# Products on parts of TensorE's array in blocks and groups, with no whole-array product inside a block

## The chip, the cores and the metric

The kernel runs on one core of a Trainium2 chip. The metric is the time of one execution in microseconds (us); lower is better. A core has five engines that each work through their own list of instructions in order: TensorE (PE) multiplies matrices, VectorE (DVE) and ScalarE (ACT) do elementwise work, GpSimd (POOL) does elementwise work and issues the gathers, SyncE (SP) issues the plain transfers. They wait for each other by semaphores only. The array of PE has 128 rows and 128 columns; a product can use all of it, or a part of 32 or 64 rows or columns (its tile size), and products on different parts can run side by side.

## The reference

One step of a hybrid decoder with DEPTH = 2 layers, for 512 prompt tokens and 8 sequences of 8 sample tokens with 2048 cached tokens each, D_MODEL = 1024. A layer is

```python
h = rms_norm(x, p["norms"][0]) * (1.0 + sc1) + sh1          # sc1, sh1, ...: silu(c) @ w_ada
nq, nkv, ngt, ucv, ret, gdn, mg = split_cols(h @ p["w_in"], IN_SPLITS)
o_nsa, new_win = nsa_attention(...)      # compressed, selected and window attention, 4 heads of 64
o_conv, new_conv = conformer_conv(...)   # depthwise convolution, 31 taps
o_ret, new_ret = retention(...)          # chunkwise, 4 heads of 64
o_gdn, ... = gated_deltanet(...)         # chunkwise delta rule, 4 heads of 64
merged = jnp.einsum('btnw,nwd->btnd', branches, p["w_branch"])
gates = jax.nn.sigmoid(mg.reshape(B, T, N_BRANCH, D_MODEL))
mixed = jnp.einsum('btnd,btnd->btd', gates, merged) @ p["w_out"]
x = x + gt1 * rms_norm(mixed, p["norms"][1])
h2 = rms_norm(x, p["norms"][2]) * (1.0 + sc2) + sh2
f, new_ffn = conv_ffn(h2, ...)           # d_ff 2816
x = x + gt2 * rms_norm(f, p["norms"][3])
```

The large products (w_in, w_branch, w_out, the ffn) are whole-array work; heads of 64, blocks of 32 and sums over rows are work on parts of the array.

## The kernel before

**Large products.** Tokens stand in two halves of 288 (512 prompt and 64 sample). Each large product is three products of split numbers, high by high, low by high and high by low (lines 346 to 348 of `mm`), with the weights as 128x128 tiles. `split_w` loads a weight tile `raw`, copies its high part `whi` on ACT (line 298) and subtracts the low part `wlo` on DVE (line 299). Such a product is called an `mm` here.

**Products on part of the array.** 4384 of the program's 18616 matmuls have a tile size smaller than 128x128: sums over rows for the norms (line 415), the pieces of the adaLN product `adaps` in four strips of 32 columns (line 383), retention (lines 833 to 855), the delta rule (1055 to 1223), and most of the attention.

**Order.** The program is written stage by stage with generators that yield between steps; at each yield some products of another stage (the gates and merges of the layer, whose operands are early) can be put between. A scheduler then fixes one static order for each engine from the dependencies, its own durations and priorities. Some helpers add dependencies that set the order only and wait for nothing at run time: `in_one_go` ties the matmuls of one `with` to the first, `after_pe` ties them behind the matmul before, `order_allocs` keeps the buffers of a tag in program order.

**The attention stage (nsa).** It comes last among the four mixers and lies between two stretches of large products; 912 `mm` of gates and merges are at hand there per layer as filling. The prompt part runs 16 steps: scores (line 1617), bias, maximum, exp and scale on DVE and ACT (1621 to 1628) for two heads in turn, transposes of `E` (1634), a copy to `ET` (621), products with the values (1641). The sample part multiplies queries with gathered pages (1662), then with window pages `kwin` (1711), runs a softmax chain `chain(G)` for each of two groups G, and `values(G)` transposes the probabilities (1792) and multiplies them with gathered pages `pg<-cv` (1802). All pages share one tag of 8 buffers; POOL issues one gather per page, 32 of them for `cv` in a layer. The stage ends with line 1813; the last merge, whose first product reads `bh`, needs its result.

Of the kernel before, what the change touches and what calls it, by code (L numbers as in the profile page):

```python
# [46 lines left out]
FCH = [(0, 7), (7, 14), (14, 22)]  # L47

# [125 lines left out]
class Kern:  # L174
    def __init__(self, ctx, tc, ap, depth=DEPTH, dbg=None, mixers=True):
# [14 lines left out]
        self.first = None  # L190

# [44 lines left out]

    def order_after(self):
# [37 lines left out]
    def turn(self, out, src, ident, p=0):  # L275

        if p:
            self.nc.tensor.matmul(out, src, ident, start=True, stop=True)
        else:
            self.nc.tensor.transpose(out, src, ident)  # L280
# [87 lines left out]
    def ada_piece(self, l, q, k, box, mod, par):  # L368
# [9 lines left out]
        def end():  # L378
            if k == 0:
                box.append(self.ax("adaps"))  # L380
            ps = box[0]
            for b in range(4):
                nc.tensor.matmul(ps[32 * b:32 * b + 32, :], self.csil[:, k, :], t[:, 512 * b:512 * b + 512],  # L383
                                 start=k == 0, stop=k == KT - 1, tile_position=(0, 32 * b))
# [5 lines left out]
            for j in range(4):  # L390
                nc.tensor.transpose(po[:, j * P:(j + 1) * P], y[:, j * P:(j + 1) * P], self.ident)
# [12 lines left out]
    def inv_rms(self, srcs, nh, scale, sel, get):  # L404
# [8 lines left out]
        for j, t in enumerate(srcs):  # L413
            for g in range(n):
                nc.tensor.matmul(th[32 * g:32 * g + 32], mat, t[:, g * w:(g + 1) * w], start=j == 0, stop=j == len(srcs) - 1,
# [10 lines left out]
        if n * w == HALF:  # L426
# [4 lines left out]
            nc.tensor.matmul(out[0][:, :HALF], self.ones, own, start=True, stop=True)  # L431
            return [out[0][:, :HALF]]
        for g in range(n):
            c = g * w
            nc.tensor.matmul(out[c // HALF][:, c % HALF:c % HALF + w], sel[:, g * P:(g + 1) * P], r, start=True, stop=True)
# [197 lines left out]
    def proj_tm(self, l, c0, n, h, dst, extra=None):  # L633
# [5 lines left out]
        for tt in range(5):  # L639
# [4 lines left out]
            for k in range(KT):  # L644
                hi, lo = ws[k // 4]
                ah, al = h[k]
                nc.tensor.matmul(o, ah[:, s], hi[:, k % 4], start=k == 0, stop=False)  # L647
                nc.tensor.matmul(o, al[:, s], hi[:, k % 4], start=False, stop=False)  # L648
                nc.tensor.matmul(o, ah[:, s], lo[:, k % 4], start=False, stop=k == KT - 1)  # L649
# [13 lines left out]
    def colsum(self, mat, srcs, hf):  # L663

        ps = self.ps("a", 4)
        for i, t in enumerate(srcs):
            self.nc.tensor.matmul(ps[:, :HALF], mat, t[:, HS[hf]], start=i == 0, stop=i == len(srcs) - 1)
# [114 lines left out]
    def retention(self, l, par, h, rv, qraw, kraw, tick):  # L782
# [4 lines left out]
        with self.phase("rrot", True):  # L787
            perm, cos, sin = self.ctile("perm"), self.ctile("cos"), self.ctile("sin")
            for raw, dst in ((qraw, q), (kraw, k)):
                for p in range(2):  # L790
# [3 lines left out]
                    for hf in range(2):  # L794
                        s = HS[hf]
                        ps = self.ps("a", 2)
                        nc.tensor.matmul(ps[:, :HALF], perm, src[:, s], start=True, stop=True)
# [6 lines left out]
        with self.phase("rchunk", True):  # L804
# [4 lines left out]
            for tt in range(5):  # L809
# [6 lines left out]
                if tt < 4:  # L816
                    for p in range(2):
                        nc.tensor.transpose(ps[:, p * P:(p + 1) * P], k[p][:, s], self.ident)
# [9 lines left out]
                with self.in_one_go():  # L828
                    for p in range(2):
                        for e in range(2):  # L830
                            b = 64 * e
                            oo = pe[e][:, p] if tt < 4 else pe[e][64 * p:64 * p + 64, 0, :SMP]
                            nc.tensor.matmul(oo, k[p][b:b + 64, s], q[p][b:b + 64, s], start=True, stop=True)
# [6 lines left out]
                if tt < 4:  # L840
                    po = self.ps("o", 1)
                    oo = lambda hd: po[64 * (hd % 2):64 * (hd % 2) + 64, hd // 2 * P:(hd // 2 + 1) * P]
                    with self.in_one_go():
                        for hd in (1, 0, 3, 2):
                            nc.tensor.matmul(oo(hd), v[:n, hd * 64:hd * 64 + 64], att[:n, self.hx(hd), :n], start=hd < 2 or tt == 0, stop=tt == 0)
                        if tt:
                            for hd in (1, 0, 3, 2):
                                p, b = hd // 2, 64 * (hd % 2)
                                nc.tensor.matmul(oo(hd), S[p][b:b + 64, :], qx[p][b:b + 64, s], start=False, stop=p == 1)
# [3 lines left out]
                    for hd in range(4):  # L853
                        p, b = hd // 2, 64 * (hd % 2)
                        nc.tensor.matmul(pS[b:b + 64, p * 64:p * 64 + 64], t[:, hd * 64:hd * 64 + 64], v[:, hd * 64:hd * 64 + 64],
# [31 lines left out]
    def on_state(self, out, x, S0, s):  # L887

        for e, p in ((0, 0), (1, 1), (0, 1), (1, 0)):
            b, c = 64 * e, 64 * p  # L890
            self.nc.tensor.matmul(out[e][c:c + 64, :], x[p][b:b + 64, s], S0[p][b:b + 64].rearrange("p b e -> p (b e)"),
# [12 lines left out]
    def sample_state(self, l, S0, dst, o, att, v, kz, q, mask, update, ps, tags=("vx0", "vx1", "oT")):  # L904
# [6 lines left out]
        for p in range(2):  # L911
            b = 64 * p
            for e in range(2):
                nc.tensor.matmul(pa[b:b + 64, e * HD:(e + 1) * HD], att[b:b + 64, e, :SMP], v[b:b + 64, e * HD:(e + 1) * HD],
# [4 lines left out]
        nc.tensor.transpose(pt[:, :P], oT, self.ident)  # L919
# [9 lines left out]
        for e, p in ((0, 0), (1, 1), (0, 1), (1, 0)):  # L929
            b, c = 64 * p, 64 * e  # L930
            nc.tensor.matmul(pS[p][c:c + 64, :], kz[b:b + 64, e * HD:(e + 1) * HD], vx[e][b:b + 64], start=True, stop=True)
# [4 lines left out]
    def gdn(self, l, par, h, tok, feed):  # L936
# [34 lines left out]
        nc.tensor.matmul(ps[:, 0:16], triu, g[:, 0:16], start=True, stop=True)  # L971
        nc.tensor.matmul(ps[:, 32:48], self.ones, g[:, 0:16], start=True, stop=True)
        for b in (0, 64):
            nc.tensor.matmul(ps[b:b + 64, 16:18], triu8[b:b + 64], g[b:b + 64, 16:18], start=True, stop=True)
            nc.tensor.matmul(ps[b:b + 64, 48:50], on8[b:b + 64], g[b:b + 64, 16:18], start=True, stop=True)
# [55 lines left out]
        with self.phase("gchunk", True):  # L1031
# [7 lines left out]
            def inverse(tt, lane):  # L1039
# [13 lines left out]
                for j, hd in enumerate(HDJ):  # L1053
                    gcol = col(g, hd) if pr else g[rows(j), 16 + j // 2:17 + j // 2]
                    nc.tensor.matmul(un(GB, j), gcol.to_broadcast([n, n]), tu[rows(j)], start=True, stop=True)
# [12 lines left out]
                for e in range(2):  # L1068
# [3 lines left out]
                    for p in range(2):  # L1072
                        r, c = rows(p), p if pr else 0
                        nc.tensor.matmul(ps[r, c, :n], k[p][b:b + 64, s], k[p][b:b + 64, s], start=True, stop=True)
                        nc.tensor.matmul(ps[r, w + c, :n], k[p][b:b + 64, s], q[p][b:b + 64, s], start=True, stop=True)
# [18 lines left out]
                def mm32(out, lhsT, rhs, r, c):  # L1094
                    nc.tensor.matmul(out, lhsT, rhs, start=True, stop=True, tile_position=(32 * r, 32 * c))  # L1095
# [40 lines left out]
                if pr:  # L1136
# [26 lines left out]
                    for j in range(4):  # L1163
                        nc.tensor.matmul(ps[h1, j], U[h0, j, h1], X64[h0, j], start=True, stop=True)
# [3 lines left out]
                    for j in range(4):  # L1168
                        nc.tensor.matmul(ps[h0, j], R[h1, j], WT[h1, j, h1], start=True, stop=True)
# [4 lines left out]
            def scan(tt):  # L1174
# [5 lines left out]
                for p in range(2):  # L1180
                    nc.tensor.transpose(ps[:, p * P:(p + 1) * P], k[p][:, s], self.ident)
                    nc.tensor.transpose(ps[:, 256 + p * P:256 + (p + 1) * P], v[p][:, s], self.ident)
# [1066 lines left out]
```

## Time and profile before

| | |
|---|---|
| median of 3 runs | 2560.45 us (2560.42 to 2568.15) |
| the profiled execution | 2563.72 us, span of its instructions 2561.9 us |
| mean granted TensorE clock | 0.988 of full speed |
| PE busy | 2446.2 us, 95% of the span, 22850 matmul records |
| DVE, ACT, POOL busy | 55%, 37%, 24% |

A share of busy time is a mean over many stages. A matmul is shown with a modelled end: an `mm` of 288 columns is shown as about 0.30 us long, though the next one starts 0.13 us after it. So for PE the distance from start to start says more than the length. A matmul in f32 is two passes and leaves two records.

### The profile page before, as it was taken

To read this page: it belongs to the slowest core of one execution; us is meant where nothing else is said; L and a number is where in the kernel's file an instruction comes from. 1 tells how busy PE (TensorE), PEld (TensorE's weight loads), DVE (VectorE), ACT (ScalarE), POOL (GpSimd) and SP (SyncE) were. 2 spreads that over 40 slices of the span, in tenths; PEclk is the share of its full clock that TensorE was granted. 3 is DMA by queue.
4 is the path that set the end of the run, shared out by engine and by line. 5 is a ranking of instruction groups with operands and counts; after the bars stand their busy time and mean duration, and the time that the engine had idled before them with its cause. 6 is when DMAs were issued, how large, how long until landed. Compare 5 with 4: busy or idle time off the path is not lost.

```text
span 2561.9 us, 54461 instructions
## 1 busy us (share of the span) xinstructions
PE 2446.2 (95%) x22850; PEld 2178.6 (85%) x22850; DVE 1411.1 (55%) x2918; ACT 938.0 (37%) x1815; POOL 613.5 (24%) x801
## 2 busy tenths in 40 slices
PE   6999999999999999999989999999999999999997
PEld 3769787976789899999977687889677999999997
DVE  5789644445524662534579884443553357444446
ACT  4316222434324543323452342233442355333233
POOL 2102322235522210101122032322635222000012
PEclk8999999999999999999999999999999999999999
DMA  8753355423634132422467433524345233233234
GB/s 313 228 195 120 111 173 196 141 89 113 198 98 156 54 120 87 144 86 83 129 216 243 139 102 128 172 80 130 108 138 172 93 117 123 84 121 109 88 89 128
DMA packets 125637, 346.78 MB, mean 135 GB/s; under 512 B 28652, under 2 KB 48112, under 8 KB 119184
## 3 DMA queue, kind: packets, MB, share of 16 engines
q1 hardware_dynamic: 104592, 275.05, 33.0%
q0 software_dynamic: 20800, 68.25, 8.3%
q8 instruction: 180, 2.95, 0.5%
q14 instruction: 65, 0.53, 0.1%
HBM read 330.77 MB, written 20.73 MB: 137 GB/s over the span
## 4 chain that ended last, share of the span: by engine, by line
PE 78%; DVE 9%; DMA 5%; ACT 3%; issue 3%; POOL 2%; SPq 0%; ACTq 0%; DVEq 0%; POOLq 0%
PE mm L346 20%; PE mm L347 20%; PE mm L348 19%; DMA pg<-cv,ix 2%; PE x L1095 2%; DVE wlo L299 2%; PE adaps L383 1%; PE cmps L1514 1%; DVE cvy L715 1%; DMA raw<-wout 1%; PE mmt L649 1%; PE mmt L647 1%; PE mmt L648 1%; PE t L1634 1%; DMA raw<-wtr 1%
## 5 line engine op out<-in xcount | busy, mean ns | idle before, releaser
L346 PE MATMUL mm<-hh,whi 128*128 128x288 f32 x3136 | 946.1, 302 | 7.3 <-ACT whi L298 4.5
L347 PE MATMUL mm<-hl,whi 128*128 128x288 f32 x3136 | 938.5, 299 | 1.2 <-DVE hl L483 1.1
L348 PE MATMUL mm<-hh,wlo 128*128 128x288 f32 x3136 | 937.5, 299 | 2.1 <-DVE wlo L299 2.1
L299 DVE TENSOR_TENSOR wlo<-raw,whi 128x1024 fp32r<-128x1024 f32 (+1 forms) x320 | 390.5, 1223 | 534.1 <-ACT whi L298 528.9
L346 PEld LDWEIGHTS mm<-hh,whi 128*128 128x128 f32 x3136 | 591.6, 189 | 36.1 <-issue 14.9
L347 PEld LDWEIGHTS mm<-hl,whi 128*128 128x128 f32 x3136 | 595.2, 190 | 15.0 <-issue 9.3
L348 PEld LDWEIGHTS mm<-hh,wlo 128*128 128x128 f32 x3136 | 592.3, 189 | 17.2 <-issue 11.6
L298 ACT ACTIVATE whi<-raw 128x1024 fp32r<-128x1024 f32 (+1 forms) x320 | 334.9, 1048 | 544.3 <-PE mm L347 354.5
L348 PE MATMUL mm<-acth,wlo 128*128 128x288 f32 x704 | 206.5, 295 | 2.1 <-DVE wlo L299 2.1
L347 PE MATMUL mm<-actl,whi 128*128 128x288 f32 x704 | 208.1, 296 | 0.0
L346 PE MATMUL mm<-acth,whi 128*128 128x288 f32 x704 | 208.0, 296 | 0.1
L576 POOL COPY nfp<-gb 128x2 f32<-128x2 f32 x44 | 42.3, 960 | 610.6 <-ACT gb L550 610.6
L1473 POOL DMA_INDIRECT pg<-ck,ix x128 | 131.1, 1024 | 102.9 <-issue 49.4
L1857 POOL TENSOR_TENSOR f<-f,gate 128x288 f32<-128x288 f32 x80 | 72.4, 919 | 291.3 <-DVE gate L1856 290.7
L348 PEld LDWEIGHTS mm<-acth,wlo 128*128 128x128 f32 x704 | 131.9, 188 | 2.9 <-DVE wlo L299 2.6
L347 PEld LDWEIGHTS mm<-actl,whi 128*128 128x128 f32 x704 | 132.9, 189 | 0.9 <-DVE actl L355 0.5
L346 PEld LDWEIGHTS mm<-acth,whi 128*128 128x128 f32 x704 | 132.2, 188 | 1.3 <-ACT acth L354 1.0
L1473 POOL DMA_INDIRECT fil<-cc,ix x64 | 69.2, 1082 | 143.9 <-PE cmps L1514 125.8
L715 DVE SCALAR_TENSOR_TENSOR cvy<-cgb,par,cvy 128x512 f32<-128x512 f32 x120 | 93.4, 791 | 0.0
L1835 ACT ACTIVATE gate<-mm 128x288 f32<-128x288 f32 x112 | 45.3, 404 | 126.0 <-PE mm L348 105.2
L346 PE MATMUL mm<-bh,whi 128*128 128x288 f32 x256 | 80.1, 315 | 1.9 <-ACT ga L1835 1.4
L347 PE MATMUL mm<-bl,whi 128*128 128x288 f32 x256 | 78.5, 307 | 2.3 <-DVE bl L355 2.3
(600 smaller groups left out, 3965.6 us busy)
## 6 DMA issues: line engine op xcount, KB each, us to landing
raw<-wtr SPq DMA_DIRECT2D x124, 512.0 KB
raw<-wup SPq DMA_DIRECT2D x104, 512.0 KB
f<-wada SPq DMA_DIRECT2D x32, 1024.0 KB
fil<-wada SPq DMA_DIRECT2D x16, 1024.0 KB
raw<-wdn SPq DMA_DIRECT2D x32, 512.0 KB
raw<-wdn SPq DMA_DIRECT2D x32, 448.0 KB
raw<-wbr SPq DMA_DIRECT2D x16, 512.0 KB
raw<-wout SPq DMA_DIRECT2D x16, 512.0 KB
```

What stands on the lines that cost most here:

```text
L298: nc.scalar.activation(hi, raw, AF.Copy)
L299: nc.vector.tensor_sub(lo, raw, hi.bitcast(F32))
L346: nc.tensor.matmul(ps, hi[:, k0 + k], ah[:, s], start=first, stop=False)
L347: nc.tensor.matmul(ps, hi[:, k0 + k], al[:, s], start=False, stop=False)
L348: nc.tensor.matmul(ps, lo[:, k0 + k], ah[:, s], start=False, stop=last)
L383: nc.tensor.matmul(ps[32 * b:32 * b + 32, :], self.csil[:, k, :], t[:, 512 * b:512 * b + 512], start=k == 0, stop=k == KT - 1, tile_positi ...
L576: nc.gpsimd.tensor_copy(newp[:, ft], g[:, SEQ:SEQ + 2])
L715: nc.vector.scalar_tensor_tensor(y[:, :SEQ], gb[:, j:j + SEQ], wj(j), y[:, :SEQ], op0=OP.mult, op1=OP.add)
L1095: nc.tensor.matmul(out, lhsT, rhs, start=True, stop=True, tile_position=(32 * r, 32 * c))
L1473: self.nc.gpsimd.indirect_dma_start(out=dst, out_offset=None, in_=self.ap[src], in_offset=bass.IndirectOffsetOnAxis(ap=ix[:, l, b, j:j + 1 ...
L1835: self.nc.scalar.activation(gts[hf], ps, AF.Tanh, scale=0.5)
L1857: nc.gpsimd.tensor_add(fm, fm, gm)
```

## The change

All matmuls and transposes outside `mm` go through two helpers, which number blocks: a block is a run of products on part of the array that stand together in the program. `issue_together` then adds dependencies that set the order only. The first product of a block stands behind every instruction of another engine that makes an operand of the block or frees its output; the rest of the block stands behind the first. The string GROUPS names 27 groups of neighbouring blocks. In a group each block's first product stands behind the operands of all blocks of the group, and the later blocks get a priority that puts them next. No work is added or taken away; both programs have 18616 matmuls.

```diff
+GROUPS = "3+7+8+9+10+11 12+13 24+26+27 50+52 56+57 68+69+74 70+71 85+86 87+88+89+90 91+92 103+105 112+113 155+157 167+168 212+228 213+214 ..."
+    def mmul(self, out, lhsT, rhs, **k):
+        with self.place(lhsT):
+            self.nc.tensor.matmul(out, lhsT, rhs, **k)
+    def place(self, held):
+        part = held.shape[0] <= 64 or math.prod(held.shape[1:]) <= 64
+        ins = self.nc.cur_bb.bb.instructions
+        if part and (len(ins) in self.cuts or not self.part(ins[-1])):
+            self.block += 1
+            part = self.block in self.later
+        return self.tc.high_priority(10 ** 6) if part else nullcontext()
+    def issue_together(self):
...
+        for group in (*self.groups, *([b] for b in sorted(alone))):
+            need = {u: None for b in group for u in needs[b]}
+            for b in group:
+                for u in need:
+                    self.tc.add_manual_dep(blocks[b][0], u, info, reason="operands of the group")
+        for first, *rest in blocks:
+            for i in rest:
+                self.tc.add_manual_dep(i, first.name, info, reason="in one go")
...
-                                self.nc.tensor.matmul(S[kv], w[rows[kv]], x[rows[kv], :nk], start=j == 0, stop=j == 2)
+                                self.mmul(S[kv], w[rows[kv]], x[rows[kv], :nk], start=j == 0, stop=j == 2)
...
+        self.issue_together()
         self.order_allocs()
```

In the changed program the helpers' lines 246 and 250 stand for all these products, and lines 346 to 348 have become 412 to 414, so rows are told apart by the names of their tiles.

PE, attention over the prompt, second block of queries, before: `s` are scores, `t<-cst,E` the transposes of the probabilities, `o<-ET` the products with the values, `mm` the filling.

```order
L1617 MATMUL s_6571<-nkh,nqh_5699 128x256 x2
L1634 MATMUL t<-cst,E 128x128 x2
L1617 MATMUL s_6571<-nkl,nqh_5699 128x256 x2
L1617 MATMUL s_6571<-nkh,nql 128x256 x2
L1634 MATMUL t<-cst,E 128x128 x2
L348 MATMUL mm<-hh,wlo 128x288
L346 MATMUL mm<-hh,whi 128x288
L347 MATMUL mm<-hl,whi 128x288
L348 MATMUL mm<-hh,wlo 128x288
L1641 MATMUL o<-ET,kvb_6106 64x128 x2
L1641 MATMUL o<-ET,kvb_6134 64x128 x2
```

The same step now:

```order
L250 MATMUL t<-cst,E 128x128 x2
L414 MATMUL mm<-hh,wlo 128x288
L412 MATMUL mm<-hh,whi 128x288
L413 MATMUL mm<-hl,whi 128x288
L414 MATMUL mm<-hh,wlo 128x288
L246 MATMUL o<-ET,kvb_6106 64x128 x2
L246 MATMUL s_6571<-nkh,nqh_5699 128x256
L246 MATMUL o<-ET,kvb_6134 64x128
L246 MATMUL s_6571<-nkh,nqh_5699 128x256
L246 MATMUL o<-ET,kvb_6134 64x128
L246 MATMUL s_6571<-nkl,nqh_5699 128x256 x2
L246 MATMUL s_6571<-nkh,nql 128x256 x2
```

Before, the scores of a step were issued while the transposes of the step before were still to come; now they stand right behind the value products of the step before, all on parts of the array.

PE, the end of the sample attention of the first layer, before: `pT` are transposed probabilities, `pg` pages, `selO` the last product of the stage.

```order
L1802 MATMUL o<-pg,pT 32x128 x2
L1792 MATMUL t<-cst,S_5630 128x128 x4
L1802 MATMUL o<-pg,pT 32x128
L348 MATMUL mm<-hh,wlo 128x288
L346 MATMUL mm<-hh,whi 128x288
L347 MATMUL mm<-hl,whi 128x288
L348 MATMUL mm<-hh,wlo 128x288
L346 MATMUL mm<-hh,whi 128x288
L1792 MATMUL t<-cst,S_5630 128x128
L1802 MATMUL o<-pg,pT 32x128 x14
```

The same products now, up to the first product of the last merge:

```order
L246 MATMUL o<-pg,pT 32x128 x16
L246 MATMUL o<-nvx,cT_8762 128x128
L246 MATMUL o<-pg,pT 32x128 x16
L250 MATMUL t<-cst,S_5630 128x128 x12
L246 MATMUL o<-pg,pT 32x128 x48
L246 MATMUL s<-selO,os 128x32 x2
L412 MATMUL mm<-bh,whi 128x288 x3
```

The value products stand whole and together, and no `mm` is left between them; before, 319 `mm` still stood between the last product of the stage and the merge, now none.

## Rows read from the trace of the kernel before

**Rows 1.** The profile's page: busy time, share of the span and instructions of each engine.

```profile
PE 2446.2 (95%) x22850; PEld 2178.6 (85%) x22850; DVE 1411.1 (55%) x2918; ACT 938.0 (37%) x1815; POOL 613.5 (24%) x801
```

**Rows 2.** Timeline of PE at 686 us: start us, length us, engine, line, tiles.

```profile
686.42 0.29 PE L347 MATMUL mm<-hl,whi 128*128 128x288 f32 x1
686.64 0.41 PE L1802 MATMUL o<-pg,pT 128*32 128x128 f32 x2
686.98 0.40 PE L348 MATMUL mm<-hh,wlo 128*128 128x288 f32 x1
687.22 0.30 PE L346 MATMUL mm<-hh,whi 128*128 128x288 f32 x1
687.35 0.29 PE L347 MATMUL mm<-hl,whi 128*128 128x288 f32 x1
```

**Rows 3.** Timeline of PE in retention, 157 to 159 us, and at 558 us.

```profile
156.86 1.05 PE L383 MATMUL adaps<-f,csl 128*32 128x512 f32 x2
157.84 0.66 PE L845 MATMUL o<-ratt,rv 128*64 128x128 f32 x8
158.42 0.65 PE L849 MATMUL o<-xi,rS 64*64 64x128 f32 x8
159.01 0.63 PE L383 MATMUL adaps<-f,csl 128*32 128x512 f32 x3
...
558.57 0.44 PE L1641 MATMUL o<-ET,kvb 128*64 128x128 f32 x4
```

**Rows 4.** Timeline of DVE and PE in one step over the prompt, 562 us.

```profile
562.02 0.43 DVE L1621 TENSOR_TENSOR s<-s,nb 128x256 f32<-128x256 f32 x1 [0.56 <-PE s L1617]
...
563.63 0.41 DVE L1621 TENSOR_TENSOR s<-s,nb 128x256 f32<-128x256 f32 x1
563.95 0.45 DVE L1628 TENSOR_SCALAR E<-E,ss,ngt 128x256 f32<-128x256 f32 x1
...
566.31 0.41 DVE L1628 TENSOR_SCALAR E<-E,ss,ngt 128x256 f32<-128x256 f32 x1
```

**Rows 5.** Windows of the attention stage: stretch, length, busy by engine, PE clock, DMA.

```profile
520.00:641.00 121.00, 113.65 (x1057) 86.15 (x1055) 63.99 (x168) 53.31 (x148) 55.94 (x59) 1.00 0.34 102
641.00:722.00 81.00, 74.68 (x700) 60.45 (x700) 41.18 (x75) 23.88 (x46) 44.68 (x45) 0.98 0.59 188
722.00:760.00 38.00, 37.96 (x287) 37.73 (x285) 8.01 (x10) 9.91 (x17) 4.22 (x3) 1.00 0.22 70
...
1972.00:2013.00 41.00, 40.96 (x309) 40.68 (x308) 9.76 (x15) 10.22 (x19) 5.82 (x5) 1.00 0.23 73
```

**Rows 6.** Timeline of POOL, the gathers for the values of the first layer.

```profile
652.10 2.38 POOL L1473 DMA_INDIRECT pg<-cv,ix  x1 [1.19 <-PE s L1711]
...
709.94 0.95 POOL L1473 DMA_INDIRECT pg<-cv,ix  x1 [0.31 <-issue]
711.19 0.95 POOL L1473 DMA_INDIRECT pg<-cv,ix  x1 [0.30 <-issue]
```

**Rows 7.** Timeline of PE: first transpose of the values, last product, last merge.

```profile
662.82 0.27 PE L1765 MATMUL t<-cst,S 128*64 128x128 f32 x1
...
720.16 0.38 PE L1813 MATMUL s<-selO,os 128*128 128x32 f32 x2
...
759.70 0.30 PE L346 MATMUL mm<-bh,whi 128*128 128x288 f32 x1
```

**Rows 8.** Windows around a stretch of low clock in the sample attention.

```profile
672.00:679.10 7.10, 3.87 (x43) 2.75 (x44) 6.79 (x9) 0.88 (x2) 5.88 (x5) 1.00 0.79 254
679.10:682.50 3.40, 3.40 (x14) 2.46 (x14) 1.99 (x1) 0.60 (x1) 2.49 (x4) 0.51 0.51 149
```

**Rows 9.** Groups of PE by line over the whole run, idle time before them.

```profile
L1802 PE MATMUL o<-pg,pT 128*32 128x128 f32 x640 | 36.7, 283 | 12.5 <-DMA pg<-cv,ix 12.1
L1634 PE MATMUL t<-cst,E 128*128 128x128 f32 x160 | 29.8, 284 | 11.1 <-DVE E L1628 9.5 <-ACT ET L621 0.5
```

**Rows 10.** Timeline of PE, the first large product of the run.

```profile
45.75 0.61 PE L346 MATMUL mm<-hh,whi 128*128 128x288 f32 x1 [3.31 <-ACT whi L298]
```

More of the change, by code (lines that the diff above doesn't have):

```diff
@@ L190, in __init__ @@
         self.first = None
+        self.cuts, self.block = set(), -1
+        self.groups = [[int(b) for b in g.split("+")] for g in GROUPS.split()]
+        self.later = {b for g in self.groups for b in g[1:]}
     def const(self, name, shape=None):
@@ new lines, in part @@
+    @staticmethod
+    def part(i):
+        return isinstance(i, mybir.InstMatmult) and tuple(i.tile_size) != (P, P)
+    def issue_together(self):
+        info = mybir.DependencyInfo(mybir.DependencyClass.NoSync, mybir.DependencyReason.SCHED_ONLY)
+        blocks, needs, along = [], [], False
+        users, tags = {}, {}
+        for n, i in enumerate(self.nc.cur_bb.bb.instructions):
+            read, written = read_tiles(i), written_tiles(i)
+            part = self.part(i)
+            if part:
+                if not along or n in self.cuts:
+                    blocks.append([])
+                    needs.append({})
+                blocks[-1].append(i)
+            along = part
+            for t in written:
+                if t.name not in users:
+                    users[t.name] = {}
+                    old = tags.setdefault(t.tag, [])
+                    bufs = t.bufs or 2
+                    if len(old) >= bufs:
+                        users[t.name].update(users[old[-bufs]])
+                    old.append(t.name)
+            for t in (*read, *written):
+                if part:
+                    needs[-1].update({u: None for e, u in users.get(t.name, {}).items() if e != i.engine})
+                users.setdefault(t.name, {})[i.engine] = i.name
+        assert self.block + 1 == len(blocks)
+        alone = set(range(len(blocks))) - {b for g in self.groups for b in g}
+        for group in (*self.groups, *([b] for b in sorted(alone))):
[6 more added lines that the diff above has]
+                self.tc.add_manual_dep(i, first.name, info, reason="in one go")
@@ L277, in turn @@
         if p:
-            self.nc.tensor.matmul(out, src, ident, start=True, stop=True)
+            self.mmul(out, src, ident, start=True, stop=True)
         else:
-            self.nc.tensor.transpose(out, src, ident)
+            self.flip(out, src, ident)
     def ax(self, name="ax"):
@@ L430, in inv_rms @@
             nc.vector.tensor_mul(own.rearrange("p (g t) -> p g t", g=n), r.unsqueeze(1).to_broadcast([P, n, w]), pick)
-            nc.tensor.matmul(out[0][:, :HALF], self.ones, own, start=True, stop=True)
+            self.mmul(out[0][:, :HALF], self.ones, own, start=True, stop=True)
             return [out[0][:, :HALF]]
@@ L434, in inv_rms @@
             c = g * w
-            nc.tensor.matmul(out[c // HALF][:, c % HALF:c % HALF + w], sel[:, g * P:(g + 1) * P], r, start=True, stop=True)
+            self.mmul(out[c // HALF][:, c % HALF:c % HALF + w], sel[:, g * P:(g + 1) * P], r, start=True, stop=True)
         return [o[:, :HALF] for o in out]
@@ L918, in sample_state @@
         pt = ps[3]()
[L919 removed]
+        self.flip(pt[:, :P], oT, self.ident)
         for p in range(2):
@@ L1054, in inverse @@
                     gcol = col(g, hd) if pr else g[rows(j), 16 + j // 2:17 + j // 2]
-                    nc.tensor.matmul(un(GB, j), gcol.to_broadcast([n, n]), tu[rows(j)], start=True, stop=True)
+                    self.mmul(un(GB, j), gcol.to_broadcast([n, n]), tu[rows(j)], start=True, stop=True)
                 yield
@@ L1094, in mm32 @@
                 def mm32(out, lhsT, rhs, r, c):
-                    nc.tensor.matmul(out, lhsT, rhs, start=True, stop=True, tile_position=(32 * r, 32 * c))
+                    self.mmul(out, lhsT, rhs, start=True, stop=True, tile_position=(32 * r, 32 * c))
                 U, X, W, WT = f4("U"), f32("X"), f32("Wc"), f4("W")
```

145 lines of the change are left out of this document (75 added, 70 removed).

## The prediction

> **What bounds the kernel now.** I read the page first, then the distances from start to start on PE, then windows of the attention stage, then POOL's timeline. The page shows PE busy for 95% of the span, no other engine above 55% [rows 1], so the question is what PE's time is made of. (PEld, the weight loads, lies beside it.) Two things in it are not products.
>
> The first is a change of tile size. At 686 us two passes on a part of the array stand between `mm`s [rows 2]. Undisturbed, one `mm` follows the other after 0.13 us (687.22 to 687.35). From 686.42 to 687.35 there are three `mm` starts, 0.40 us of work, and two passes. A pass over 128 columns takes 0.11 us: L1641 and L845 run in pairs, side by side, and two pairs are shown 0.44 us long, four pairs 0.66, so a pair adds 0.11 [rows 3]. That makes 0.62 us of work in 0.93 us, so one trip away from the whole array and back costs **0.31 us**. Changing from one part size to another costs too: L845 and L849 are four pairs each, 0.45 us of work, and take 0.58 and 0.59 us to the next start [rows 3]. So such a change costs about **0.13 us**. Both are small and numerous.
>
> The second is waiting, which collects in few places: before the transposes of `E`, 11.1 us, mostly for DVE's scaling, and before the value products, 12.5 us, mostly for gathered pages [rows 9]. Both lie in the attention stage.
>
> **What the change does, part by part.** It removes and adds no work, so every term is a change of order.
>
> *Trips saved.* I counted the changes of tile size along both PE orders, leaving out the `mmt` products. Whole to part and back: 425 trips before, 293 after. Part to part: 157 before, 295 after. If only trips cost, the gain would be 132 x 0.31 = 41 us; with the other changes paid, it is 41 - 138 x 0.13 = 23 us. I take the second, since [rows 3] show the price directly. The Trainium skill, page "TensorEngine Tiling (Array Packing)", section "Key Properties", says that changing the tiling mode, not merely the tile, drains TensorE. It speaks against counting trips alone, and the 0.13 us agree with it; by it, all changes alike at 0.155 us, half a trip, give (1007 - 881) x 0.155 = 20 us.
>
> Outside the attention stage the counts are 274 trips to 220 and 103 to 123 part-to-part changes: 54 x 0.31 - 20 x 0.13 = 14 us. There is a second gain: a strip product that was cut off from its neighbours no longer runs alone. One `adaps` product by itself held PE for 0.98 us, about 0.87 without the step [rows 3], and six such cuts disappear; most lie in retention, where another engine can be the limit, so I count 4 us of them. Together **-18 us** (-14 to -24).
>
> *The attention stage.* Its trips fall from 151 to 73 while its part-to-part changes rise from 54 to 172: 24.2 - 15.3 = 9 us in two layers, and 15 lone passes of L1802 less are 3 us more: 6 us per layer. But the order changes more than that, and I work it out for the first layer.
>
> A block of the program holds the value products of one step and the scores of the next. Now the block stands together, behind the operands of both. The scores of the next step no longer run ahead, so each of the 16 steps has its full chain: the first head's bias to its scaled `E` is 562.02 to 564.40, 2.4 us; the second head's started 1.6 us later and ended at 566.72 [rows 4], so some 4 to 4.7 us, then transposes, a copy of 0.4 us, and the product, 5 to 5.5 us. For that time the order holds 33 to 37 `mm`, 4.4 to 4.9 us, and the transposes. So a step waits 0.2 to 0.6 us; I take 6 us in all (3 to 10).
>
> These `mm` are taken from the end. Before, the stage's last product ran at 720.16 and the merge began at 759.70 [rows 7]; the 38 us from 722 to 760 are filled with 287 products and nothing else [rows 5]. That stock covers nothing of the attention: it is work left over. After the change the 912 `mm` are used up before the values of the sample part: 690 in the prompt steps, and 168 directly between the first window product of the second group and its other three. What follows, the tail, runs bare.
>
> When does the tail start? PE was busy for 113.65 + 74.68 + 37.96 = 226.3 us between 520 and 760 [rows 5]. Some 7 us of that are, by my estimate, short waits, hidden because an `mm` is shown 0.29 us long while the next can start after 0.13 [rows 2]. Of the 219 us, 6 are saved by fewer changes. About 19 are the tail's own products: 160 value products, four side by side, and 40 transposes, in two passes each, are 80 x 0.11 + 80 x 0.11, and a few others. So 194 us come before it. With 6 us of waits in the steps it starts at 520 + 200 = **720 us** (712 to 728).
>
> How long is the tail? POOL issues a gather every 1.25 us (709.94 to 711.19), and the last one, at 711.19, was followed by the stage's last product until 720.54 [rows 6, 7]: 9.4 us for landing, products and the closing sums. Page buffers come free only when the second group's window products are done, so 31 of 32 gathers lie in the tail: 31 x 1.25 + 9.4 = 48 us, and 49 with what else POOL does there. It can be shorter if three more gathers get ahead (45 us). In the trace of before the same part, from 662.82 to 720.54, took 58 us with `mm` between [rows 6, 7]; that is the upper end. So the merge starts at 720 + 49 = 769 us instead of 759.7: **+9 us per layer**, +18 in all. The second layer has the same shape, 41 us of pure filling at its end [rows 5]. Ends: 712 + 45 = 757, where the tail is hidden and PE's saved 6 us per layer are the gain (-12 in all); and, at the other end, 728 + 58 = 786, +26 per layer (+52).
>
> *Other shifts.* At the start the norm of the second half of the tokens goes behind the adaLN pieces, and its row products on DVE now come between the modulation and the first `mm`. That product waited for ACT's `whi`, 3.3 us, at 45.75 us [rows 10], so part of a delay is hidden: +1 us (0 to 3). In retention the first chunk waits for some 50 `mm` and the chunks then have little filling, +1.5 us per layer (0 to 3). Together +4 us.
>
> The sum is -18 + 18 + 4 = **+4 us**. The profiled execution, 2563.7 us, becomes 2567.7; it lies 3.3 us above the median of the runs, so against 2560.45 I expect **2564.5 us**.
>
> **The rivals.** *The tail is hidden.* If the short waits in PE's busy time are more than 7 us, or the chain of a step is covered by its 33 to 37 `mm`, the tail starts at 712 or earlier; from a tail start near 710 us with 49 us of tail the stage ends no later than before, and each earlier microsecond counts until PE's saved 6 us are reached. Then the sum is -18 - 12 + 4 = -26 at best and about -17 halfway: 2534 to 2552, middle 2543. For it speaks that L1634's waits were only 11.1 us in 32 steps [rows 9]; against it that nothing runs ahead any more.
>
> *The tail is longer, and runs into the low clock.* With 58 us from 725, a layer ends at 783, 23 us late. Then -18 + 46 + 4 = +32; halfway to the forecast it is +20: 2580 to 2595, middle 2585. It decides from a tail start plus length of about 774 us. For it speaks the trace: after 7.1 us with PE busy for 3.87, the granted clock was 0.51, the 1.2 GHz level, for 3.4 us [rows 8], and in the bare tail PE has 19 us of work in 49. The clock alone adds half of 3.4 us to the merge, 1.7 us per layer. The Trainium skill, page "TensorE: Matmul & The Clock Gate", section "Part 1: The HAM clock gate", says that an idle array falls to half its clock and gets it back after having been busy; [rows 8] show the fall.
>
> *Only trips cost.* If a change between part sizes were free and the 0.13 us of [rows 3] had another cause, the gain outside the attention stage would be 54 x 0.31 + 4 = 21 us, and the stage would save 78 x 0.31 + 3 = 27 us in two layers, 13.6 per layer instead of 6. Its tail would start at 712.4 and end at 761.4, 1.7 us late per layer: -21 + 3 + 4 = -14, 2547 us.
>
> **How the numbers follow.** The forecast gets 0.40, the hidden tail 0.28, the long tail 0.26, trips alone 0.06. Runs of this kernel tell 0.3%, 7.7 us, from no change: below 2552.8 is faster, above 2568.1 slower. The forecast's own range is 2554 to 2576, from the spread of its small terms; of its 0.40 about 0.02 lie below, 0.25 between and 0.13 above. The hidden tail and trips alone lie below, 0.01 of the long tail between and the rest above. That is faster 0.36, same 0.26, slower 0.38. To leave out 2 in 10, the range cuts a tenth at each side: 2538 to 2590.
>
> **What would show it.** PE's distances at a trip stay 0.31, and there are fewer of them. In the prompt steps PE waits before the transposes of `E` for DVE, more than 11.1 us in total. POOL's gathers for `cv` start only after 712 us, stand at 1.25 us without pauses, and PE's busy share in their window falls below a half, with no `mm` between the last value product and the merge at about 769 us. The prediction is wrong if gathers begin much earlier, if the order of the steps hides the chain, or if retention or the start move by more than 3 us.

## The result, and the profile after

The changed kernel takes 2586.05 us (median of 6 runs, 2581.26 to 2590.71), the kernel before, in the same comparison, 2567.76 us (6 runs, 2560.42 to 2579.62). The ratio is 1.0069, 95% interval [1.004, 1.0098]: slower. The profiled execution took 2584.99 us, with a span of 2582.8 us against 2561.9 and a mean granted clock of 0.970 against 0.988.

The page of the kernel after, busy time:

```profile
PE 2452.0 (95%) x22850; PEld 2197.3 (85%) x22850; DVE 1412.8 (55%) x2918; ACT 937.4 (36%) x1815; POOL 615.0 (24%) x801
```

PE's busy time hardly moved against [rows 1]: shares of the whole span show nothing of a loss that sits in two places. Windows of the attention stage of the first layer do, after (columns as in [rows 5]):

```profile
520.00:682.00 162.00, 160.46 (x1356) 132.03 (x1361) 73.61 (x182) 61.70 (x159) 69.90 (x70) 1.00 0.32 98
682.00:717.80 35.80, 35.80 (x286) 32.80 (x271) 19.58 (x40) 12.96 (x27) 3.61 (x3) 1.00 0.44 143
717.80:780.00 62.20, 42.97 (x408) 28.29 (x405) 19.34 (x35) 14.06 (x27) 35.19 (x35) 0.65 0.55 165
780.00:784.00 4.00, 4.00 (x16) 3.95 (x17) 2.35 (x4) 0.83 (x2) 0.36 (x1) 0.50 0.01 4
```

Up to 717.80 PE is full at full clock. Then come 62 us in which it is shown 43 us busy at a mean clock of 0.65, the bare tail of the prediction, and the last merge begins at half clock. In [rows 5] the stretch from 722 to 760 was full at 1.00. PE in that tail, after:

```profile
717.80 0.27 PE L250 MATMUL t<-cst,S 128*64 128x128 f32 x1
...
729.35 1.90 PE L246 MATMUL o<-pg,pT 128*32 128x128 f32 x26 [1.69 <-DMA pg<-cv,ix]
...
746.24 0.64 PE L246 MATMUL o<-pg,pT 128*32 128x128 f32 x2 [2.06 <-DMA pg<-cv,ix]
...
779.28 0.63 PE L246 MATMUL s<-selO,os 128*128 128x32 f32 x2 [0.29 <-ACT no L688]
779.99 1.09 PE L412 MATMUL mm<-bh,whi 128*128 128x288 f32 x3
...
781.43 0.44 PE L412 MATMUL mm<-bh,whi 128*128 128x288 f32 x1
781.67 0.44 PE L413 MATMUL mm<-bl,whi 128*128 128x288 f32 x1
```

The last two rows show the price of the clock: `mm` start 0.24 us apart, not 0.13. The merge begins at 779.99; in [rows 7] it began at 759.70.

To see where the time went over the whole run, take the start of the same `mm` (the n-th in order of time) in two traces and follow the difference. Against the trace of before, in us; the last four columns are kernels of the experiments, one trace each:

| stretch | after | change, a third time | attention free | half gathers | half, same depth |
|---|---|---|---|---|---|
| to the attention of layer 1 | -0.9 | +1.0 | +1.6 | +2.3 | -1.3 |
| attention of layer 1 | +19.8 | +22.6 | +0.4 | +0.2 | -1.3 |
| between | -11.5 | -11.9 | -11.7 | -17.5 | -19.5 |
| attention of layer 2 | +15.2 | +17.8 | -4.8 | +0.1 | -5.8 |
| to the end | -1.8 | -0.7 | -2.0 | +0.1 | -0.3 |
| all | +20.8 | +28.8 | -16.5 | -14.8 | -28.2 |

Outside the attention the change gives 14 us; in it, it loses 35. (Outside it the same order gives 11.6 us in the third trace of the change, and the other three columns 12.1, 15.1 and 21.1: so much do single traces differ.)

### The profile page after: what moved, and what is told of

It reads as the page before. It is cut to its first block, busy times and chain, and to the rows that moved or that the text cites. A ratio compares the mean times of both kernels' runs of the same rounds, so it can differ in the third digit from the quotient of the medians.

```text
span 2582.8 us, 54446 instructions
## 1 busy us (share of the span) xinstructions
PE 2452.0 (95%) x22850; PEld 2197.3 (85%) x22850; DVE 1412.8 (55%) x2918; ACT 937.4 (36%) x1815; POOL 615.0 (24%) x801
## 4 chain that ended last, share of the span: by engine, by line
PE 77%; DVE 9%; DMA 6%; ACT 3%; issue 3%; POOL 1%; SPq 0%; ACTq 0%; DVEq 0%; POOLq 0%
PE mm L412 20%; PE mm L413 19%; PE mm L414 19%; PE x L246 3%; PE o L246 3%; PE mmt L246 2%; DVE wlo L365 2%; PE s L246 2%; DVE cvy L782 2%; PE a L246 1%; DMA pg<-cv,ix 1%; PE cmps L246 1%; PE t L250 1%; ACT whi L364 1%; DMA raw<-wtr 1%
## 5 line engine op out<-in xcount | busy, mean ns | idle before, releaser
L412 PEld LDWEIGHTS mm<-hh,whi 128*128 128x128 f32 x3136 | 591.8, 189 | 28.8 <-issue 7.6
L1924 POOL TENSOR_TENSOR f<-f,gate 128x288 f32<-128x288 f32 x80 | 80.1, 1017 | 226.8 <-DVE gate L1923 226.3
L1540 POOL DMA_INDIRECT pg<-cv,ix x64 | 68.4, 1068 | 100.2 <-PE s L246 68.4
```

The costliest lines, as they stand in the source:

```text
L412: nc.tensor.matmul(ps, hi[:, k0 + k], ah[:, s], start=first, stop=False)
L1540: self.nc.gpsimd.indirect_dma_start(out=dst, out_offset=None, in_=self.ap[src], in_offset=bass.IndirectOffsetOnAxis(ap=ix[:, l, b, j:j + 1 ...
L1924: nc.gpsimd.tensor_add(fm, fm, gm)
```

## The experiments

The theory after the result: the loss is the bare tail of the sample attention, it exists because the blocks of the prompt attention use up the filling, and its length is POOL's gathers plus waits that the prediction left out. Rivals: the whole value blocks of the sample part, the groups, or the low clock alone.

The first and the second batch (four kernels each) ran on two chips that took about 2670 us for the kernel before; in the first comparison and in the third batch it took about 2565. Ratios are compared within a batch; where batches are set side by side, the chip differs.

Most kernels loosen some blocks. `FREE` is the set of loose block numbers; groups with such a block are dropped:

```diff
-        for group in (*self.groups, *([b] for b in sorted(alone))):
+        for group in (*self.groups, *([b] for b in sorted(alone - FREE))):
...
-        for first, *rest in blocks:
+        for first, *rest in (x for b, x in enumerate(blocks) if b not in FREE):
```

### First batch: which part of the change (before: 2669.26 us)

**Only the attention blocks.**

```diff
+FREE = set(range(441)) - {*range(170, 224), *range(381, 435)}
```

> Blocks and groups only in the attention stage of both layers; everywhere else the order is left to the scheduler as before. Theory (all of the loss is in the attention stage, 20 and 15 us, and the rest gains 14): 33 to 37 us slower than the kernel before. Rival (something outside the stage, retention or the start, loses, and the attention loses less): less than 25 us slower.

Measured: 2717.7 us, ratio 1.0178 [1.0148, 1.0208]. The attention alone brings the whole loss. Without the gain outside it should lie 14 us further from its kernel before than the change does; it is 48 us, and the change in the second batch 44, each to within some 10 us, so that gain isn't told here.

**Sample part loose.** The whole value blocks of the sample part are undone.

```diff
+FREE = {*range(202, 224), *range(413, 435)}
```

> The change as it is, except that the sample part of the attention (window products, value products) has no block and no group. Theory of the serial prompt steps: the filling is used up in the prompt all the same, so the run stays where the change is, 15 to 22 us slower than before. Rival of the whole value blocks: their products start page by page again, the end of the stage is back to before, and the run is 10 us or more faster than before.

Measured: 2717.11 us, ratio 1.0176 [1.0149, 1.0204], like the change itself on the chip of the second batch (below). So whole value blocks are not the cause.

**Prompt blocks cut.** Only the prompt attention's blocks are cut, wherever the tag of the output tile changes: the value products of a step no longer wait for the operands of the next step's scores, nor the scores for the value products.

```diff
+SPLIT = FREE = {*range(170, 202), *range(381, 413)}
...
+                if number in SPLIT:
+                    if out != written[0].tag:
+                        parts.append([])
+                        wants.append({})
+                        out = written[0].tag
+                    parts[-1].append(i)
...
+        for (first, *rest), w in zip(parts, wants):
+            for u in w:
+                self.tc.add_manual_dep(first, u, info, reason="operands of the group")
```

> The change as it is, except that in the attention over the prompt a block ends where the output tile changes: value products of one step, scores of the next and sample scores are blocks of their own, each still whole and behind its own operands only. Theory (the merged blocks make the steps serial, the steps use up the filling, and the rest of the attention runs bare): the scores run ahead again, the last value product of the prompt is back near 636 us, filling is left at the end of the stage, and the whole run is 14 to 24 us faster than the kernel before (about 2545 beside 2562). Rival (the value products of the sample part, whole and behind all their pages, make the end of the stage long): the stage still ends 10 us or more late per layer and the run is not faster than before.

Measured: 2659.89 us, ratio 0.9965 [0.9947, 0.9982]: faster than before. Everything else of the change stands in it.

**Blocks without groups.**

```diff
-GROUPS = "3+7+8+9+10+11 12+13 24+26+27 ..."
+GROUPS = ""
```

> All blocks whole and behind their operands, but no groups (the list is empty). There are 310 trips and 285 part-to-part changes in place of 294 and 297. By the prices of 0.31 and 0.13 us that is 3 us more than the change. Theory: 18 to 26 us slower than before, since the loss comes from the blocks, not from the groups. Rival (the groups cause delays at the start, in retention and in the delta rule that cost what the blocks gain there): at least 5 us faster than the change.

Measured: 2706.49 us, ratio 1.0155 [1.0123, 1.0186]. It loses too, so the groups are not needed for the loss; the interval overlaps the change's, so what the groups are worth isn't told.

The signs came as expected, the sizes did not: 48 us slower for the attention alone (33 to 37 expected), 48 with the sample part loose (15 to 22), 37 without groups (18 to 26), and 9 us faster with the prompt blocks cut (14 to 24). The change itself costs 44 us on the chip of the next batch, not 18.

### Second batch: the clock in the tail (before: 2671.65 us)

**The kernel before and the change, again.** Unaltered, as the measure on this chip.

> The kernel before, unchanged, for a profile from the same chip as the runs beside it. No theory parts on it.

> The change, unchanged, beside the others on one chip. On the chip of the first comparison it was 0.69% slower. If this chip lets the engines wait for each other as long as that one, the same again, 0.4 to 1.0% slower; if it is the chip on which blocks without groups were 1.55% slower, then 1.4 to 1.9% slower.

Measured: 2668.06 us (one run) and 2715.45 us, ratio 1.0172 [1.0128, 1.0215].

**Warm tail.** Ten f32 whole-array products of the identity with itself, result unused, ahead of the products of each value block.

```diff
                 vp = vps.pop(0)
+                warm = self.ax("warm")
+                with self.after_pe():
+                    for _ in range(10):
+                        nc.tensor.matmul(warm[:, :P], self.ident, self.ident, start=True, stop=True)
```

> The change with 100 more products per layer (128x128 by 128 columns, f32, 0.22 us each, results unused): ten stand behind the transposes of each value block of the sample attention, so PE has 22 us more to do in the stretch without filling. Theory (the low clock makes the stretch longer: value blocks at half speed release the pages late, so the gathers pause): the granted clock there stays nearer to 1.0, the stretch shrinks from 62 us towards 52, and the run is 5 to 20 us faster than the change although it does more. Rival (gathers alone pace the stretch, the low clock costs nothing there): the run is the same as the change or up to 10 us slower.

Measured: 2707.47 us, ratio 1.015 [1.0118, 1.0182], 8 us below the change though it does more; the two intervals overlap, so that it is faster isn't shown. Windows of its first tail, and of the change's on the same chip:

```profile
785.10:800.00 14.90, 14.80 (x174) 12.44 (x177) 8.86 (x17) 4.81 (x10) 10.68 (x11) 1.00 0.58 165
...
810.00:820.00 10.00, 8.53 (x113) 7.20 (x111) 2.85 (x6) 3.67 (x8) 5.40 (x6) 1.00 0.84 254
820.00:830.00 10.00, 9.01 (x119) 7.79 (x115) 0.00 (x0) 1.19 (x2) 6.69 (x7) 1.00 0.63 177
```

```profile
800.00:810.00 10.00, 8.03 (x76) 4.88 (x77) 8.60 (x12) 2.14 (x5) 6.92 (x7) 0.66 0.61 169
810.00:820.00 10.00, 2.88 (x35) 1.35 (x34) 0.00 (x0) 1.69 (x2) 3.88 (x5) 0.78 0.71 226
820.00:830.00 10.00, 8.33 (x77) 6.19 (x77) 2.78 (x8) 2.13 (x6) 4.34 (x5) 0.50 0.38 106
```

In the first layer the warm tail keeps the clock at 1.00 up to 840 us and lasts from 785.17 to 845.96, 60.8 us; the change's lasts from 789.16 to 854.48, 65.3 us. In the second layer the two last 58 and 60 us. The change's own first tails last 62.2, 65.3 and 65.2 us in its three traces. So the warm products give back some 2 to 4 us per layer, net of the work that they add. 58 to 61 us stay at a clock near 1.00, and the kernel before needs 58 for the same part: most of the tail is something else than the clock. The expected shrinking towards 52 us did not come.

**Prompt blocks cut, again.** The same kernel as in the first batch.

> The change with the blocks of the prompt attention cut where the output tile changes, beside the change itself on one chip. Theory (merged blocks cost 20 and 15 us and the 14 us outside the stage remain): faster than the kernel before by 0.3 to 0.9%, and faster than the change by 1.0 to 2.2%. Rival (part of the loss is elsewhere): less than 0.8% faster than the change.

Measured: 2659.73 us, ratio 0.9959 [0.9936, 0.9982]. Its attention stage of the first layer, windows: before the first value transposes of the sample part, up to the stage's last product, and from there to the last merge:

```profile
580.00:708.90 128.90, 101.72 (x841) 74.55 (x842) 61.98 (x148) 47.00 (x120) 56.53 (x59) 0.85 0.36 110
708.90:768.00 59.10, 49.02 (x526) 39.05 (x525) 22.26 (x38) 15.35 (x28) 33.97 (x35) 0.96 0.56 169
768.00:827.70 59.70, 57.28 (x425) 56.16 (x424) 16.01 (x19) 16.53 (x29) 10.03 (x8) 1.00 0.21 67
```

The sample part takes 59 us here too, but it is over early, and 60 us of whole-array products are left behind it, some 420 `mm`. (In the kernel before 294 stand behind the stage's last product; 319 are counted from its last value product.)

### Third batch: the length of the tail, and the gain outside (before: 2562.64 us)

**Attention free.** All blocks of the attention are loose.

```diff
+FREE = {*range(170, 224), *range(381, 435)}
```

> The changed kernel with the blocks of the attention stage left loose, so that only the blocks and groups outside the stage are held together. The sum's terms for what lies outside the stage, -18 us of tile changes and +4 us of other shifts, give -14 us against the kernel before: a ratio of about 0.995, seen where the norms and retention lie and not inside the stage. The rival, that the groups outside the stage also cost more than they give once the stage follows the order of before, gives 1.000 or above.

Measured: 2546.25 us, ratio 0.9938 [0.9923, 0.9954]: 16.4 us faster than before.

**Half gathers**, in two forms. The selected pages of every second sequence are left out; the neighbour's are used in their place. In the second form, where the three added lines stand behind `page_tile()`, their buffers were to be taken in turn all the same and stay empty.

```diff
                     b = 4 * G + b4
+                    if qi < 4 and b4 % 2:
+                        vps.append(vps[-1])
+                        continue
                     vp = self.page_tile().rearrange("p (a n) -> p a n", a=4)
```

> The changed kernel, with half of the value pages of the sample part left out: every second sequence multiplies with the pages of its neighbour, so 16 gathers for the values per layer in place of 32, each page buffer serving two sequences, and the eight buffers reach twice as far. If the length of the tail is POOL's spacing of 1.25 us per gather and the waits for a free buffer, the tail loses 16 x 1.25 = 20 us and most of its 8.6 us of such waits, over 20 us per layer, and the ratio falls by about 0.015 to 0.02 against the changed kernel's. If the tail is the chain of transposes, copies, products and softmax at the low clock, the tail loses under 8 us per layer and the ratio falls by less than 0.006.

> As the kernel with half of the value gathers, but the buffers of the pages that are left out are still taken in turn and stay empty, so that the buffers reach no further ahead than in the changed kernel; the same part of the attention is left out. If POOL's spacing alone sets the tail, this is as fast as the kernel with half of the gathers. If the waits for free buffers and the time in which a page lands set it, this one lies between that kernel and the changed one, at least 5 us per layer above the first.

Measured: 2547.88 us, ratio 0.9945 [0.9931, 0.996], and 2541.25 us, ratio 0.9927 [0.9911, 0.9944].

**The change, a third time**, as their measure.

> The changed kernel once more, as the measure for the two kernels with half of the gathers on the chip of these runs: 1.007 on the chip of the first comparison, 1.017 on the chip of the later runs, with tails of 62 and 65 us in the first layer.

Measured: 2591.88 us, ratio 1.0113 [1.0098, 1.0127], more than on the chip of the first comparison; its tail in the first layer lasts 65.2 us. Half of the gathers less saves 22 us per layer, and 25 in the second form, for 16 gathers at 1.26 us each: the tail goes by the number of gathers. Transfers don't queue up behind them: a gather of the tail lands as fast in the changed kernel, 31 of them, as in the first form, 15:

```profile
DMA to landing us min/median/max: 3.4/3.6/5.2
DMA to landing us min/median/max: 3.3/3.8/6.2
```

The second form does not test the reach of the eight buffers. In its trace:

```profile
726.98 1.08 PE L247 MATMUL o<-pg,pT 128*32 128x128 f32 x32
728.08 3.25 SPq L1853 DMA_DIRECT2D pg<-vwin  x4
731.93 1.08 PE L247 MATMUL o<-pg,pT 128*32 128x128 f32 x32 [0.75 <-ACT pT L689]
```

With all eight buffers taken in turn, the window pages `vwin` of the second group would need the buffers of the first group's third gathered block, whose products begin at 731.93. They are loaded from 728.08, right behind the products of the first gathered block (726.98), as they are in the first form. So the empty buffers were not held: both forms gather the same pages in the same order with the same reach, the 6.6 us between them are what two runs of that order differ by, and the expected 5 us per layer stay untested.

But the tail of the first layer is still 42.7 us with half of the gathers (720.96 to 763.69, first form), where 15 intervals of 1.26 and the closing 9.4 would give 28. More than half of what stays is seen in POOL's timeline of this kernel:

```profile
742.58 0.97 POOL L1541 DMA_INDIRECT pg<-cv,ix  x1 [0.31 <-issue]
745.18 0.53 POOL L1560 MEMSET kvc<- 128x512 f32 x1 [1.64 <-PE o L247]
752.04 0.98 POOL L1541 DMA_INDIRECT pg<-cv,ix  x1 [6.33 <-issue]
753.32 0.95 POOL L1541 DMA_INDIRECT pg<-cv,ix  x1 [0.30 <-issue]
```

No gather starts for 9.5 us in the middle, and for 6.33 of them the profile names no releaser. The same place in the changed kernel, from its first profile:

```profile
742.45 0.96 POOL L1540 DMA_INDIRECT pg<-cv,ix  x1 [0.30 <-PE o L246]
743.45 0.31 POOL L1835 MEMSET cT<- 64x256 f32 x1
749.15 0.96 POOL L1540 DMA_INDIRECT pg<-cv,ix  x1 [5.39 <-PE o L246]
...
752.94 0.96 POOL L1540 DMA_INDIRECT pg<-cv,ix  x1 [0.30 <-PE s L246]
753.93 0.53 POOL L1559 MEMSET kvc<- 128x512 f32 x1
757.38 0.96 POOL L1540 DMA_INDIRECT pg<-cv,ix  x1 [2.92 <-PE o L246]
...
771.24 0.95 POOL L1540 DMA_INDIRECT pg<-cv,ix  x1 [0.30 <-issue]
```

This is the turn from the first group of four sequences to the second. From the last gather of the first group to the fifth of the second are five intervals: 14.9 us here instead of 6.3. Here the releaser is named: the gathers wait for buffers that value products (`o`) free, first for the first group's last pages, then for the second group's window pages, and these products wait in turn for pages and copies.

## Why the prediction was right and wrong

The time lies in the range given, and slower was the side with the larger chance, 0.38. But the likeliest case, 2564.5 us, missed by 21.5: what came is the second rival, the longer tail that runs into the low clock, with 2585 us. That the time lies so near to 2585 is luck in part: the rival had the tail start at 725 and last 58 us, and in the first layer it started at 717.8 and lasted 62.2 (in the second it lasted 60).

**Outside the attention: right as a sum.** The terms were -18 and +4, together -14; the table gives -0.9 - 11.5 - 1.8 = -14.2. The price of a trip stands. A lone part product between `mm`s, after:

```profile
694.25 0.29 PE L414 MATMUL mm<-hh,wlo 128*128 128x288 f32 x1
694.46 1.05 PE L246 MATMUL s<-pg,qb 128*32 128x512 f32 x2
695.44 0.40 PE L412 MATMUL mm<-hh,whi 128*128 128x288 f32 x1
695.68 0.29 PE L413 MATMUL mm<-hl,whi 128*128 128x288 f32 x1
```

From 694.25 to 695.68 are 1.43 us; two `mm` starts of 0.13 and 0.87 for the lone product leave 0.30. Spread was off: the start and the mixers of the first layer gave 1 us in this trace and other traces lie on either side of zero, while 6.2 us come between the layers, where sums for a norm had stood in four pieces. The same sums now, after:

```profile
1307.67 0.33 PE L246 MATMUL nr<-accy,ones 128*32 128x72 f32 x8
1307.82 0.68 PE L246 MATMUL nr<-sq,ones 128*32 128x72 f32 x24
1308.43 0.40 PE L413 MATMUL mm<-actl,whi 128*128 128x288 f32 x1
```

Of these 6.2 us the trips explain about 2: the two traces have 11 and 4 of them there. The same stretch (1275 to 1334 before, 1291.6 to 1344 after) has 2.8 us less of idle time on PE, which no term of the sum held.

The kernel with the attention left free was to show -14 and shows -16.4, some 5 us of it in the second layer's attention in its one trace; so the -14 holds as a sum, not place by place.

**The waits in the steps: wrong, and small.** I gave 6 us per layer to steps whose scores no longer run ahead, and wrote that PE would wait more than the 11.1 us of [rows 9] before the transposes of `E`. It waited 0.8 us, in both layers together:

```profile
L250 PE MATMUL t<-cst,E x160: 270/273/328, 539.9 to 1940.9; 128*128 128x128 f32 x160
its engine sat idle before it (us, times) until:
  DVE E L1695: 0.8, 4
```

The `mm` placed in each step cover the chain, one of the signs of being wrong that the prediction named. That is also where they go: the prompt steps hold 343 more of them and end 45 us later (681.5 against 636.7), 343 x 0.133 = 45.6.

**The start of the tail: right.** 717.80 against 720; 31 of the 32 gathers lie in it, as said. But the sum had 6 us of waits in it that did not come; without them it gives 714, so its other terms were 3 to 4 us too small, and the two errors balance.

**The length of the tail: the step that failed.** "31 x 1.25 + 9.4 = 48" took one spacing for all gathers and counted the wait for landing and products once, at the end. Measured are 62.2 us. They are 1.6 to the second gather (the first had got ahead at 695.78), 30 intervals of 1.26, 8.6 more at the turn between the groups, 1.9 where POOL has other work and then waits, ahead of the gather at 725.87, 3.4 for gathers that issued longer than 0.95 us, and 8.75 behind the last one. The turn was there before: its five intervals take 13.7 us in the trace of before (683.62 to 697.34), 7.4 too many, with `mm` beside them and 3.2 us of POOL's own gating work in them:

```profile
683.62 0.95 POOL L1473 DMA_INDIRECT pg<-cv,ix  x1 [0.30 <-issue]
...
685.00 1.56 POOL L1857 TENSOR_TENSOR f<-f,gate 128x288 f32<-128x288 f32 x2
689.46 0.97 POOL L1473 DMA_INDIRECT pg<-cv,ix  x1 [2.89 <-PE o L1802]
...
697.34 0.97 POOL L1473 DMA_INDIRECT pg<-cv,ix  x1 [0.16 <-issue]
```

I had 58 us for the same part with `mm` between and put it down as the upper end, as though the filling made it long. It was the better estimate. In the kernel with the attention free, this part takes 60 us too.

**The low clock: right as a mechanism, its price in the tail left out.** I gave it 1.7 us per layer, for the merge. There it held: the merge ran at half clock from 779.99 to about 784, which costs 2 us (the merge before had its own stretch at 0.62 and 0.53, from 764 to 768). In the tail I gave it nothing. Rows of the tail, after:

```profile
735.00:745.00 10.00, 5.84 (x67) 3.45 (x67) 2.35 (x1) 2.63 (x3) 6.89 (x8) 0.73 0.65 194
745.00:758.00 13.00, 9.78 (x85) 6.94 (x89) 2.78 (x8) 2.13 (x6) 4.98 (x6) 0.50 0.50 164
```

At the turn the granted clock is 0.50, the 1.2 GHz level, and a value block of 32 records takes 1.94 us, not 1.08. Such a block after, and one before at full clock:

```profile
755.19 1.94 PE L246 MATMUL o<-pg,pT 128*32 128x128 f32 x32
...
695.77 1.08 PE L1802 MATMUL o<-pg,pT 128*32 128x128 f32 x32
```

In the first layer the warm tail has a shorter turn, 12.5 us for its five intervals where the change has 16.7 (807.87 to 820.34 in the warm kernel, 813.54 to 830.20 in the change), about as much as its tail is shorter. In the second layer it has not: 12.3 us, and 11.3 in the change. So some 4 us of the first tail are what the full clock gave back, net of the added products; more isn't shown. Also, PE is shown busy for 69% of the tail, where I said under a half: at half clock the same work is shown longer. The Trainium skill, page "TensorE: Matmul & The Clock Gate", section "HAM oscillation — how this bites in real kernels", tells of a kernel whose waits for transfers between short runs of products return the array to half its clock time after time; the windows above agree, with 0.73 and 0.50.

**Why there is a tail at all: shown.** Cut only the blocks of the prompt attention and the loss is gone, with 60 us of filling left at the end of the stage; loosen only the sample part and it stays. Between the first and the last `o<-ET` of the first layer stand 291 `mm` before, 600 in the change, and 212 with the prompt blocks cut. A block that waits for the operands of two steps draws `mm` forward into every step, and they are missing later.

**Rivals.** The hidden tail falls with the start at 717.80 and a length that no order shown here, before's 58 us included, brings down to the 49 of the sum while all pages are gathered. Trips alone had the tail start at 712.4, 5 us early. Its -17 us outside the attention lies too near to the measured -14.2 and -16.4 to be told from them, but the price that it denies is there, after:

```profile
157.84 0.66 PE L246 MATMUL o<-ratt,rv 128*64 128x128 f32 x8
158.33 0.42 PE L246 MATMUL s<-rv,rkz 128*64 128x64 f32 x8
...
160.57 0.66 PE L246 MATMUL o<-ratt,rv 128*64 128x128 f32 x8
161.15 0.65 PE L246 MATMUL o<-xi,rS 64*64 64x128 f32 x8
```

The same eight records take 0.49 us to the next start where the tile size stays and 0.58 where it changes to another part size, so such a change costs about 0.1 us.

## What to carry to other kernels

Where independent work fills the waits of several stages, a rule that makes an early stage wait tidily spends it there; look at what the last stage before a join has left, and at how long that stage is by itself. The length of such a stage is read best from its own run in the trace, stops included, and not built from its fastest spacing: a stop that is covered now is a cost when its cover is gone. Holding products on parts of the array together pays (16 us here, 0.6%), if blocks aren't joined across operands that come at different times: the kernel with the attention free, 2546 us, beats both kernels, and so does the one with only the prompt blocks cut.

## What the runs showed that I had not expected

On the chips of the first two batches the change cost 1.7% (measured on the second), not 0.7 to 1.1. There ACT's copies `ET` waited on a releaser that the profile calls remote, in every kernel: 8.1 us before, 18.5 in the change, 45.4 with the prompt blocks cut, and none in the traces of the first comparison and of the third batch. In the change the granted clock there was 0.86 from 577 us to the start of the tail at 789, where it was 1.00 in the first comparison's profile. What these waits are, no run here tells, and whether they alone make the larger ratio stays open.

A gather in the tail takes 0.95 us and 0.30 of pause for POOL most of the time, but now and then 1.3 to 2.2 us; the sum, 3.4 us in the first layer's tail, has no releaser in the profile either. And which of the waits at the turn between the groups ends last in other orders was read from timelines, not tried.
